# Roots of a group norm passed on through DRAM rows, for three of four groups

## Chip, cores and metric

One core of a Trainium2 chip runs the kernel. The metric is the device time of one execution in microseconds (us); lower is better.

## What is computed

Two layers (DEPTH = 2) of a hybrid decoder on 256 tokens of width 1024, in float32. Each layer normalises the stream, multiplies it by one wide input matrix, runs three token mixers in parallel (a Mamba-2 scan, sliding-window attention, forgetting attention), projects each to width 1024, merges them with sigmoid gates, multiplies by an output matrix and adds the result to the stream. The change sits at the end of the Mamba-2 mixer: its 1024 output channels, already multiplied by SiLU(z), are normalised in four groups of 256 channels, for each token by itself.

```python
SEQ = 256
SSM_GROUPS = 4

def grouped_rms_norm(y, w, groups):
    b, s, d = y.shape
    yf = y.astype(jnp.float32).reshape(b, s, groups, d // groups)
    yf = yf * lax.rsqrt(jnp.mean(yf * yf, axis=-1, keepdims=True) + NORM_EPS)
    return (yf.reshape(b, s, d) * w.astype(jnp.float32)).astype(y.dtype)
...
    y = y + d_skip.reshape(SSM_GROUPS, SSM_HEADS_PER_GROUP)[:, :, None] * xh
    y = y.reshape(b, s, SSM_INNER) * jax.nn.silu(z)
    return grouped_rms_norm(y, norm_w, SSM_GROUPS)
...
        branch = jnp.einsum('bsiw,iwd->bsid', ys, w_proj[layer])
```

## The kernel before

**Weights.** All of a layer's matrix products are made from a high and a low half of each operand, both in a rounded float32 format: three products, high by high, low by high, high by low. SP's queue brings weights in pieces of 128 partitions by 1024 values (`load_to`, L341). ScalarE rounds a piece into its high half and VectorE subtracts that to get the low half (`split`, L264 and L265); in the profile these are `hi<-raw` and `lo<-raw,hi`. Six buffers hold high halves and six low ones; a split waits until TensorE has released a buffer.

**Order of the work.** TensorE's order is written out by hand: a list of operations (`ops`), each a column block of a weight matrix, and between them small tasks written as generators. A task ends each stage with `yield D`, which says how long after the present moment its next stage may be issued, by a count of TensorE's time that the kernel keeps for itself (`clock`); `pump` issues the ripe stages, and `drain` issues all that is left of a task before an operation that needs it. Apart from the first operations, only TensorE's order is held to the program: the order on VectorE, ScalarE and GpSimd is chosen by the framework's scheduler when the program is built.

**The group norm.** The Mamba-2 output lies channel by channel in eight blocks of 128 channels (`y.xs`, block 0 to 7; block u holds channels on the partitions and 256 tokens along a row). Group g is blocks 2g and 2g + 1. For each block, `u_z` (L776 on) makes the gate z with 24 products, 256 wide, and multiplies it in: ScalarE's tanh (L782), VectorE's two products (L789, L790), ScalarE's square (L792); for every second block VectorE adds the two squares (L795) and launches `group_norm`.

`group_norm` sums the squares over channels with two products against two columns of ones (L803), which puts token on the partitions: 128 partitions, two values (one for each half of the tokens), each twice. GpSimd takes a power of -1/2 (L808), and VectorE refines the root (L810, L811, L813; tile `rs`). The root is now needed along the row of every partition. ScalarE multiplies the identity matrix by it (L816, two diagonals), and `D_GN2` later TensorE multiplies 128 x 128 ones by those diagonals (L820, tile `mx<-L,ones`), so that each partition holds all 256 roots in PSUM. VectorE multiplies both blocks by it and by the weight (L823), and `split` makes the high and low half (`y.yh`, `y.yl`).

**What comes next.** After block 7 TensorE makes the branch's gate, in two halves of 128 tokens (t = 0 and 1, 24 products each, 512 wide). VectorE adds a bias to each (L890), ScalarE takes a tanh (L891). Then comes the projection of the branch (`u_proj2`): both token halves, with the channel blocks 0 to 3 first and 4 to 7 after; for each block three products, high by high, low by high, high by low. Groups 0 and 1 are drained before its first product (`drain(3)`), groups 2 and 3 before its second half (`drain(4)`). `split_late` prepares the third branch's halves in four steps on ScalarE and VectorE (`L` of 512 values).

## Time and profile before

| | us |
|---|---|
| median of three runs | 848.38 |
| the three runs | 847.70, 848.38, 850.29 |
| span of the profiled execution | 846.0 |
| TensorE busy | 833.7 (99%) |
| VectorE busy | 642.3 (76%) |
| ScalarE busy | 511.6 (60%) |
| mean granted TensorE clock | 0.996 |

The span runs from the first to the last instruction of one profiled execution; the page gives no other time for that execution, and the timed runs are others. PE is TensorE's matmuls, PEld its weight loads, DVE VectorE, ACT ScalarE, POOL GpSimd and SP the engine that issues the weights' transfers; a `q` behind an engine's name marks its instruction queue, where transfers are issued. A row of the groups shows line, engine, operation, out<-in, shape and count, then the busy time in us and the mean ns of one, then idle time ahead of it. A row of the timeline begins with start and length in us and ends, in brackets, with the idle time ahead of it and what ended it. A row on transfers ends with the KB of each and the median us from issue to landing. Layer 0's group norm lies between 303 and 336 us of the span, layer 1's between 716 and 750.

### The profile page before, as it was taken

How to read it: one execution, taken by the hardware profiler on the slowest of the kernel's cores; microseconds unless marked ns; L12 is line 12 of the kernel's file. 1: busy time of each engine (PE TensorE's matmuls, PEld its weight loads, DVE VectorE, ACT ScalarE, POOL GpSimd, SP SyncE). 2: the span in 40 equal slices, each digit the busy share in tenths (PEclk: the TensorE clock that was granted, in tenths of full speed). 3: DMA queues.
4: the chain of work that ended last, by engine and by line, in shares of the span. 5: the costliest groups of instructions: out<-in, count | busy, mean ns of one | idle time of the engine just before them, and what ended most of it. 6: DMA issues, size and time to landing. Idle time of an engine off the chain costs nothing.

```text
span 846.0 us, 15985 instructions
## 1 busy us (share of the span) xinstructions
PE 833.7 (99%) x5964; PEld 763.4 (90%) x5964; DVE 642.3 (76%) x1403; ACT 511.6 (60%) x1004; POOL 105.7 (12%) x134
## 2 busy tenths in 40 slices
PE   8999999999999999999999999999999999999996
PEld 7989898998999998888989998899899999988896
DVE  5777997998776669656788879879968567785665
ACT  6466777665666667435555667776557667654442
POOL 6410100000140010210014001000003110121000
PEclk9999999999999999999999999999999999999999
DMA  9576565666465545748676465465755654576632
GB/s 303 160 226 197 180 199 163 197 212 184 143 188 177 181 145 189 230 147 292 206 237 218 144 204 157 145 200 182 239 172 176 174 175 152 161 236 211 212 100 76
DMA packets 126638, 158.43 MB, mean 187 GB/s; under 512 B 12784, under 2 KB 88224, under 8 KB 126560
## 3 DMA queue, kind: packets, MB, share of 16 engines
q1 hardware_dynamic: 109456, 140.79, 52.5%
q10 hardware_dynamic: 17056, 16.49, 6.3%
q8 instruction: 47, 0.77, 0.4%
q14 instruction: 31, 0.25, 0.1%
q0 software_dynamic: 48, 0.13, 0.0%
HBM read 155.22 MB, written 2.16 MB: 186 GB/s over the span
## 4 chain that ended last, share of the span: by engine, by line
PE 95%; DMA 3%; DVE 1%; ACT 0%; POOL 0%; issue 0%; SPq 0%; POOLq 0%; DVEq 0%
PE mm L96 82%; PE mx L96 9%; PE mx L100 4%; DMA raw<-in_w_in_dram 3%; DVE lo L265 0%; POOL lo L1154 0%; ACT hi L1153 0%; DVE L L470 0%; ACT L L1013 0%; DVE L L265 0%; ACT L L264 0%; POOLq L1218 0%; ACT L L215 0%; DVE L L996 0%; DVE L L1001 0%
## 5 line engine op out<-in xcount | busy, mean ns | idle before, releaser
L265 DVE TENSOR_TENSOR lo<-raw,hi 128x1024 fp32r<-128x1024 f32 x252 | 308.3, 1235 | 93.8 <-ACT hi L264 84.6
L96 PE MATMUL mm<-hi,L 128*128 128x512 f32 (+1 forms) x1344 | 373.9, 364 | 2.0 <-ACT hi L1153 1.5
L264 ACT ACTIVATE hi<-raw 128x1024 fp32r<-128x1024 f32 x252 | 263.4, 1056 | 93.5 <-PE mm L96 75.5
L96 PE MATMUL mm<-L,hi 128*128 128x256 f32 x1792 | 317.7, 278 | 0.7 <-DVE L L473 0.7
L96 PEld LDWEIGHTS mm<-L,hi 128*128 128x128 f32 x1792 | 277.7, 192 | 7.6 <-issue 3.3
L96 PEld LDWEIGHTS mm<-hi,L 128*128 128x128 f32 x1344 | 241.5, 190 | 32.5 <-issue 2.7
L96 PE MATMUL mm<-L,lo 128*128 128x256 f32 x896 | 246.4, 275 | 0.0
L96 PE MATMUL mm<-lo,L 128*128 128x512 f32 (+1 forms) x672 | 241.4, 361 | 0.6 <-POOL lo L1154 0.6
L96 PEld LDWEIGHTS mm<-L,lo 128*128 128x128 f32 x896 | 171.9, 192 | 0.2
L96 PEld LDWEIGHTS mm<-lo,L 128*128 128x128 f32 x672 | 127.3, 190 | 15.4 <-POOL lo L1154 0.8
L867 POOL TENSOR_SCALAR_AFFINE_SELECT bias<-bias 128x128 f32<-128x128 f32 x64 | 35.9, 597 | 407.5 <-DVE L L736 268.6
L561 ACT ACTIVATE pp<-pp,nm 128x128 f32<-128x128 f32 (+1 forms) x128 | 56.5, 443 | 13.5 <-DVE nm L555 13.5
L698 DVE SCALAR_TENSOR_TENSOR L<-L,vec,L 128x255 f32<-128x255 f32 (+2 forms) x96 | 46.3, 482 | 4.7 <-ACT L L695 3.4
L96 PE MATMUL mx<-L,L 128*64 128x128 f32 (+1 forms) x384 | 34.4, 314 | 0.0
L891 ACT ACTIVATE L<-L 128x512 f32<-128x512 f32 x24 | 15.1, 631 | 29.9 <-DVE L L890 29.7
L573 DVE TENSOR_SCALAR pp<-pp,rsum 128x128 f32<-128x128 f32 (+1 forms) x128 | 32.2, 316 | 0.5
L701 ACT ACTIVATE L<-L 128x256 f32<-128x256 f32 x32 | 13.3, 417 | 31.5 <-DVE L L698 25.9
L96 PEld LDWEIGHTS mx<-L,L 128*64 128x64 f32 x384 | 23.0, 136 | 9.4 <-ACT pp L561 1.3
L782 ACT ACTIVATE L<-mm 128x256 f32<-128x256 f32 x48 | 18.1, 378 | 20.8 <-PE mm L96 20.8
L590 ACT ACTIVATE L<-mx 128x512 f32<-128x512 f32 x48 | 27.0, 597 | 2.7 <-PE mx L100 2.5
L100 PE MATMUL mx<-ident,pp 128*128 128x128 f32 x192 | 26.3, 273 | 0.0
L555 DVE CUSTOM_DVE_ANT_0 pp<-mx,wmask,nsink 128x128 f32<-128x128 f32 x64 | 23.4, 412 | 1.5 <-PE mx L96 1.5
(173 smaller groups left out, 717.5 us busy)
## 6 DMA issues: line engine op xcount, KB each, us to landing
raw<-in_w_in_dram SPq DMA_DIRECT2D x200, 512.0 KB, 4.5
raw<-in_w_proj_dram SPq DMA_DIRECT2D x48, 512.0 KB, 5.5
raw<-in_w_out_dram SPq DMA_DIRECT2D x16, 512.0 KB, 4.6
L<-cumd ACTq DMA_DIRECT2D x8, 512.0 KB, 5.0
bias<-cumd ACTq DMA_DIRECT2D x16, 256.0 KB, 4.0
L<-in_gate_bias_dram ACTq DMA_DIRECT2D x12, 256.0 KB, 3.9
L<-in_x_dram SPq DMA_DIRECT2D x2, 512.0 KB, 4.9
nwb<-in_norm_w_dram SPq DMA_DIRECT2D x1, 512.0 KB, 5.3
```

What stands on the lines that cost most here:

```text
L96: nc.tensor.matmul(o, a, b, **kw)
L100: nc.tensor.transpose(o, a, i)
L264: keep(act)(hi, src, AF.Copy)
L265: keep(tt)(lo, src, hi.bitcast(F32), op=ALU.subtract)
L555: nc.vector.tensor_tensor_reduce(out=pp[:, i, sl], in0=score(p, i, b), in1=biases(p, i, b), scale=-0.125, scalar=1.0e30 if ns is None else ...
L561: act(pp[:, i, sl], pp[:, i, sl], AF.Exp, scale=-1.0, bias=nm[:, e:e + 1], accum_out=sums[:, e:e + 1])
L573: ts(pp[:, i, sl], pp[:, i, sl], rs[:, 2 * i + b:2 * i + b + 1], 0.5, op0=ALU.mult, op1=ALU.mult)
L590: act(pT, pt, AF.Copy)
L698: stt(a[:, s:S], x_[:, 0:S - s], y.vec[:, 16 * j + u:16 * j + u + 1], a[:, s:S], op0=ALU.mult, op1=ALU.add)
L782: act(halves(th), p, AF.Tanh, scale=0.5)
L867: nc.gpsimd.affine_select(out=bias[:, i, dst], in_=bias[:, i, src], compare_op=ALU.is_ge, fill=NEG, base=0, pattern=[[-1, P]], channel_mul ...
L891: act(g, g, AF.Tanh, scale=0.5)
```

## The change

Groups 0, 1 and 2 (`ROWS`) no longer make the diagonals and the products with ones. The root's two columns (one value of each pair) are written to a DRAM row of 2 x 128 values, and this row is read back onto all 128 partitions, in an SBUF tile of the kind that held the diagonals. Both transfers are issued from ScalarE's queue. Three delays take the place of `D_GN2`: `D_GNW` ahead of the write, `D_GNR` ahead of the read, `D_GNS` ahead of the product that uses it. Group 3 stays as it was.

```diff
+D_GNW, D_GNR, D_GNS, ROWS = 4.5, 3.5, 5.0, (0, 1, 2)
...
         stt(r[:, 0:4], a[:, 0:4], -3.0, r0[:, 0:4], op0=ALU.add, op1=ALU.mult)
-        rb = T("L1", [P, S])
-        for t in range(2):
-            act(rb[:, t * P:(t + 1) * P], ident, AF.Copy, scale=r[:, 2 * t:2 * t + 1])
-        yield D_GN2
-        p = pmx()
-        for t in range(2):
-            mm(p[:, t * P:(t + 1) * P], ones, rb[:, t * P:(t + 1) * P], start=True, stop=True)
+        if g in ROWS:
+            row = dr.tile([2, P], F32, name=f"gn{y.l}_{g}", tag=f"gn{y.l}_{g}")
+            rc = r[:, 0:4].rearrange("p (t two) -> p t two", t=2)[:, :, 0]
+            yield D_GNW
+            with nc.allow_non_contiguous_dma(reason="one column of roots"):
+                nc.scalar.dma_start(row.rearrange("t p -> p t"), rc)
+            yield D_GNR
+            rb = T("L1", [P, S])
+            nc.scalar.dma_start(rb, row.rearrange("t p -> (t p)").partition_broadcast(P))
+            yield D_GNS
+            scale = rb
+        else:
+            rb = T("L1", [P, S])
+            for t in range(2):
+                act(rb[:, t * P:(t + 1) * P], ident, AF.Copy, scale=r[:, 2 * t:2 * t + 1])
+            yield D_GN2
+            p = pmx()
+            for t in range(2):
+                mm(p[:, t * P:(t + 1) * P], ones, rb[:, t * P:(t + 1) * P], start=True, stop=True)
+            scale = p[:, 0:S]
         for u in (2 * g, 2 * g + 1):
             n = T("L1", [P, S])
-            stt(n, y.xs[:, u, :], y.vec[:, 80 + u:81 + u], p[:, 0:S], op0=ALU.mult, op1=ALU.mult)
+            stt(n, y.xs[:, u, :], y.vec[:, 80 + u:81 + u], scale, op0=ALU.mult, op1=ALU.mult)
             split(y.yh[0][:, :, u, :], y.yl[0][:, :, u, :], halves(n))
```

Line numbers of the changed kernel are one higher up to the root (L264 becomes L265), and 14 higher behind the norm (L823 becomes L837, L890 becomes L904); the write is L820, the read L823. On TensorE three rows a layer are gone (groups 0, 1 and 2), and nothing else moves. On SP and GpSimd nothing moves. On VectorE and ScalarE the scheduler chose another order around the norm, the same one in both layers.

First place: VectorE, layer 0, between the two weight pieces that are split behind block 6. `L_368` is `y.xs`; L790 (L791 after) is the product that multiplies the gate into block 6 or 7, `lo` a weight's low half, L795 (L796) the sum of the squares of blocks 6 and 7. Before:

```order
L789 TENSOR_SCALAR L_816_4244<-L_815_4242,mm_4217 128x256
L810 TENSOR_TENSOR sm_4267<-sm_4265,sm_4263 128x4
L790 TENSOR_TENSOR L_368_1837<-L_368_1837,L_816_4244 128x256
...
L789 TENSOR_SCALAR L_835_4314<-L_834_4312,mm_4275 128x256
L790 TENSOR_TENSOR L_368_1837<-L_368_1837,L_835_4314 128x256
L265 TENSOR_TENSOR lo_4407<-raw_4079,hi_4406 128x1024
L795 TENSOR_TENSOR L_817_4247<-L_817_4247,L_836_4317 128x256
```

After:

```order
L811 TENSOR_TENSOR sm_4253<-sm_4251,sm_4249 128x4
L812 TENSOR_TENSOR sm_4253<-sm_4253,sm_4251 128x4
L790 TENSOR_SCALAR L_814_4240<-L_813_4238,mm_4213 128x256
L814 TENSOR_SCALAR rs_4256<-sm_4253,sm_4251 128x4
L791 TENSOR_TENSOR L_368_1837<-L_368_1837,L_814_4240 128x256
L266 TENSOR_TENSOR lo_4363<-raw_4061,hi_4362 128x1024
L790 TENSOR_SCALAR L_829_4298<-L_828_4296,mm_4259 128x256
L266 TENSOR_TENSOR lo_4375<-raw_4079,hi_4374 128x1024
L791 TENSOR_TENSOR L_368_1837<-L_368_1837,L_829_4298 128x256
L796 TENSOR_TENSOR L_815_4243<-L_815_4243,L_830_4301 128x256
```

Group 2's root products (L811, L812) moved ahead of block 6's gating, and the second weight's low half moved ahead of block 7's product.

Second place: VectorE, layer 0, the norm's product of groups 0 and 1 (L823, after L837) and their low halves (`L_752`), beside the low halves of the weights that follow. Before, group 0 and group 1:

```order
L823 TENSOR_SCALAR L_819_4252<-L_368_1837,vec_658,mx_4249 128x256
L823 TENSOR_SCALAR L_820_4256<-L_368_1837,vec_658,mx_4249 128x256
L813 TENSOR_SCALAR rs_4270<-sm_4267,sm_4265 128x4
L265 TENSOR_TENSOR lo_4395<-raw_4061,hi_4394 128x1024
L265 TENSOR_TENSOR L_752_3939<-L_819_4252,L_751_3938 128x2x128
L265 TENSOR_TENSOR L_752_3939<-L_820_4256,L_751_3938 128x2x128
...
L823 TENSOR_SCALAR L_838_4323<-L_368_1837,vec_658,mx_4320 128x256
L823 TENSOR_SCALAR L_839_4327<-L_368_1837,vec_658,mx_4320 128x256
L265 TENSOR_TENSOR L_752_3939<-L_838_4323,L_751_3938 128x2x128
L265 TENSOR_TENSOR L_752_3939<-L_839_4327,L_751_3938 128x2x128
L890 TENSOR_TENSOR L_842_4358<-mm_4333,L_840_4331 128x512
```

After:

```order
L266 TENSOR_TENSOR lo_4397<-raw_4162,hi_4396 128x1024
L837 TENSOR_SCALAR L_850_4382<-L_368_1837,vec_658,L_833_4320 128x256
L837 TENSOR_SCALAR L_851_4386<-L_368_1837,vec_658,L_833_4320 128x256
L837 TENSOR_SCALAR L_859_4417<-L_368_1837,vec_658,L_835_4338 128x256
L266 TENSOR_TENSOR lo_4409<-raw_4180,hi_4408 128x1024
L266 TENSOR_TENSOR L_752_3939<-L_850_4382,L_751_3938 128x2x128
L266 TENSOR_TENSOR L_752_3939<-L_851_4386,L_751_3938 128x2x128
L904 TENSOR_TENSOR L_858_4414<-mm_4355,L_831_4305 128x512
L266 TENSOR_TENSOR L_752_3939<-L_859_4417,L_751_3938 128x2x128
L837 TENSOR_SCALAR L_860_4421<-L_368_1837,vec_658,L_835_4338 128x256
L266 TENSOR_TENSOR lo_4465<-raw_4276,hi_4464 128x1024
L266 TENSOR_TENSOR L_752_3939<-L_860_4421,L_751_3938 128x2x128
```

Both groups moved from ahead of the gate's first sum (L890, after L904) to behind the next weights' low halves; blocks 0 and 1 stand behind `lo_4409`, block 3 behind the gate's second sum and `lo_4465`. Behind these rows come `lo_4477`, the products of group 3, block 4's product, group 3's low halves, `lo_4501` and only then block 4's low half.

Third place: ScalarE, layer 0, from block 6's tanh on. L816 are the diagonals, L792 (L793) the squares. Before:

```order
L782 ACTIVATE L_815_4242<-mm_4217 128x256
L792 ACTIVATE L_817_4247<-L_368_1837 128x256
L264 ACTIVATE hi_4394<-raw_4061 128x1024
L264 ACTIVATE L_751_3938<-L_819_4252 128x2x128
L264 ACTIVATE L_751_3938<-L_820_4256 128x2x128
L816 ACTIVATE L_826_4272<-ident_71,rs_4270 128x128 x2
L782 ACTIVATE L_834_4312<-mm_4275 128x256
L264 ACTIVATE hi_4406<-raw_4079 128x1024
```

After:

```order
L783 ACTIVATE L_813_4238<-mm_4213 128x256
L820 DMA gn_2_4258<-rs_4256 128x2x1
L793 ACTIVATE L_815_4243<-L_368_1837 128x256
L265 ACTIVATE hi_4362<-raw_4061 128x1024
L783 ACTIVATE L_828_4296<-mm_4259 128x256
L265 ACTIVATE hi_4374<-raw_4079 128x1024
L793 ACTIVATE L_830_4301<-L_368_1837 128x256
L823 DMA L_833_4320<-gn_0_4101 128x256
L823 DMA L_835_4338<-gn_1_4202 128x256
L905 ACTIVATE L_834_4335<-L_834_4335 128x512
L265 ACTIVATE hi_4396<-raw_4162 128x1024
```

Group 2's write stands ahead of block 6's square, the reads of groups 0 and 1 behind block 7's square, and the rounding of their blocks has moved behind two more weight splits.

## Prediction

> **What bounds the kernel now.** I read the page first, for the span, the busy shares and the chain that ended last.
>
> ```profile
> span 846.0 us, 15985 instructions
> PE 833.7 (99%) x5964; PEld 763.4 (90%) x5964; DVE 642.3 (76%) x1403; ACT 511.6 (60%) x1004; POOL 105.7 (12%) x134
> PE 95%; DMA 3%; DVE 1%; ACT 0%; POOL 0%; issue 0%; SPq 0%; POOLq 0%; DVEq 0%
> ```
>
> TensorE is idle for 846.0 - 833.7 = 12.3 us in all, and 95% of the chain is its own work. So a matmul taken out is worth its whole length, and a wait put into TensorE's stream costs its whole length: nothing later has slack to win it back. The page gives only the span of the profiled execution; the median of the timed runs, 848.4 us, lies 2.4 us above it, and I carry this 2.4 over unchanged.
>
> Second view: the groups of TensorE's instructions, shapes kept apart, and its timeline around layer 0's group norm. Of the timeline's columns the first is the start, the second the length, both in us.
>
> ```profile
> L96 PE MATMUL mx<-L,ones 128*128 128x128 f32 x32 | 4.9, 275 | 0.0
> ...
> 314.25 0.61 PE L96 MATMUL mx<-L,ones 128*128 128x128 f32 x4
> 314.70 0.51 PE L96 MATMUL mx<-ones,L 128*128 128x2 f32 x4
> ...
> 317.83 0.61 PE L96 MATMUL mx<-L,ones 128*128 128x128 f32 x4
> 318.19 0.68 PE L96 MATMUL mm<-hi,L 128*128 128x512 f32 x2
> ...
> 323.46 0.61 PE L96 MATMUL mx<-L,ones 128*128 128x128 f32 x4
> 323.90 0.51 PE L96 MATMUL mx<-ones,L 128*128 128x2 f32 x4
> 324.27 0.68 PE L96 MATMUL mm<-hi,L 128*128 128x512 f32 x2
> ...
> 329.53 0.59 PE L96 MATMUL mm<-hi,L 128*128 128x512 f32 x2
> 329.96 0.38 PE L96 MATMUL mm<-lo,L 128*128 128x512 f32 x1
> 330.18 0.59 PE L96 MATMUL mm<-hi,L 128*128 128x512 f32 x2
> ...
> 332.12 0.61 PE L96 MATMUL mx<-L,ones 128*128 128x128 f32 x4
> ...
> 335.16 0.59 PE L96 MATMUL mm<-hi,L 128*128 128x512 f32 x2
> ```
>
> There are 32 records for 16 products (two records each), two products a group, eight groups in two layers. The first three rows of four records are groups 0, 1 and 2, the row at 332.12 is group 3, which stays. The row at 329.53 is the first product of the branch's projection, 335.16 the start of its second half; three 512-wide products take 0.65 us (329.53 to 330.18), so 0.216 each.
>
> **What is removed.** From the start of each product row to the row behind it: 0.45 (314.25 to 314.70), 0.36 (317.83 to 318.19), 0.44 (323.46 to 323.90). That is **1.25 us a layer, 2.5 us in all**, 0.30% of the time; 24 of 32 records of 4.9 us would be 3.7, but records overlap, so the starts count. The other order of TensorE's work does not change. ScalarE also loses three pairs of copies a layer (0.69 a pair); it is no bound by itself, and nothing is booked for them.
>
> **What is added, and its unknown durations.** Each of six groups gets a write of 256 separate four-byte values and a read of one 1 KB row onto 128 partitions, both on ScalarE's queue.
>
> ```profile
> L<-xres ACTq DMA_DIRECT2D x4, 128.0 KB, 4.0
> L<-xres ACTq DMA_DIRECT2D x2, 256.0 KB, 2.9
> ...
> dsk<-in_d_skip_dram ACTq DMA_DIRECT2D x4, 2.0 KB, 9.2
> cumd<-L ACTq DMA_DIRECT2D x2, 32.0 KB, 2.1
> ...
> L259 ACTq DMA_DIRECT2D dsk<-in_d_skip_dram x4: 621/646/646, 31.5 to 364.5; - x4
> ...
> L681 ACTq DMA_DIRECT2D cumd<-L x2: 324/334/344, 74.3 to 489.8; - x2
> ...
> DMA to landing us min/median/max: 2.1/4.0/5.9
> ```
>
> The write lands after between 2.1 (the row cumd, also into DRAM, long pieces) and 9.2 (dsk, 512 four-byte values, but among eleven transfers issued together). I take 5.6, halfway, since here are half as many values and alone. Issuing it holds ScalarE's sequencer 0.33 (cumd) to 0.65 (dsk); I take 0.65, the row with small pieces. The read: between 2.9 (L<-xres, 256 KB) and 5.9 (the longest of the accesses to cumd, in the last row); I take 4.0, the row of the same size. The norm's product on VectorE now reads its scale from SBUF, for 0.43 a piece (0.86 for two at 322.95 below) as before: a product of the same width from SBUF, L790, takes 0.42.
>
> Neither transfer is waited for at these values. Group 1's write, issued at 315.6, lands at 321.2, and the read behind it is reached at about 323.0: cover 1.8. Group 0's read, issued at 322.65, lands at 326.65, and VectorE reaches its product at 327.45: cover 0.8.
>
> The Trainium skill, page "DMA: Bandwidth & Descriptors", section "Specifications", asks for 512 bytes a transfer for line rate and says that smaller ones become read-modify-writes; that speaks against this write. The same page's section on the anatomy of a DMA gives about 2.0 us fixed cost, mostly the receipt of the write. The row cumd agrees with the second; by it alone the sum below stays as it is, and the first is one way into rival C.
>
> **What is moved.** This is the larger part: VectorE and ScalarE take their work in another order around the norm, and I lay the rows' durations end to end in the new order, on the clock of before. Their rows, in start and length:
>
> ```profile
> 315.58 1.01 POOL L808 TENSOR_TENSOR sm<-sm,mhalf 128x4 f32<-128x4 f32 x1 [2.63 <-DVE sm L805]
> ...
> 316.45 0.42 DVE L789 SCALAR_TENSOR_TENSOR L<-L,mm 128x256 f32<-128x256 f32 x1 [1.02 <-ACT L L782]
> ...
> 316.91 0.42 DVE L790 TENSOR_TENSOR L<-L,L 128x256 f32<-128x256 f32 x1
> ...
> 321.14 0.42 DVE L790 TENSOR_TENSOR L<-L,L 128x256 f32<-128x256 f32 x1
> 321.48 1.22 DVE L265 TENSOR_TENSOR lo<-raw,hi 128x1024 fp32r<-128x1024 f32 x1
> 322.62 0.42 DVE L795 TENSOR_TENSOR L<-L,L 128x256 f32<-128x256 f32 x1
> 322.95 0.86 DVE L823 SCALAR_TENSOR_TENSOR L<-L,vec,mx 128x256 f32<-128x256 f32 x2
> ...
> 317.42 0.42 ACT L792 ACTIVATE L<-L 128x256 f32<-128x256 f32 x1 [1.00 <-DVE sm L811]
> 317.79 1.06 ACT L264 ACTIVATE hi<-raw 128x1024 fp32r<-128x1024 f32 x1
> ...
> 321.68 0.41 ACT L792 ACTIVATE L<-L 128x256 f32<-128x256 f32 x1
> ...
> 325.39 0.63 ACT L891 ACTIVATE L<-L 128x512 f32<-128x512 f32 x1 [1.12 <-DVE L L890]
> ...
> 326.23 1.04 ACT L264 ACTIVATE hi<-raw 128x1024 fp32r<-128x1024 f32 x1
> ```
>
> *Wait 1, before group 3's sums.* Group 2's root products now stand ahead of block 6's gating product and wait for GpSimd until 316.6 (315.58 + 1.01); the gating product starts at 317.0 instead of 316.45. ScalarE then issues group 2's write (root at 317.5, 0.65 us) ahead of block 6's square, which moves from 317.42 to 318.15, and the weight split behind it from 317.79 to 318.5. On VectorE a low half of 1.14 us (start to start, 321.48 to 322.62) now stands ahead of block 7's product: 322.2 instead of 321.14. Its square runs at 322.65 instead of 321.68, and the sum of squares, done at 323.04 before, at 323.5. TensorE wanted it at 323.90 and now wants it 1.25 earlier, at 322.65: **0.9 us**. TensorE is then 0.35 ahead of before.
>
> *Wait 2, block 0's low half, the second product of the projection.* The projection starts at 329.53 - 0.35 = 329.2. Group 0 had its product at 317.32 before; now it stands behind the gate's weight splits: ScalarE's first split there at 325.2, its low half 326.3 to 327.45, three norm products to 328.65, another low half to 329.8, then block 0's low half, done at 330.2. TensorE wants it at 329.4: **0.8 us**.
>
> *Wait 3, block 3.* VectorE goes on without a gap: block 1 to 330.5, the gate's sum (0.6) to 331.1, block 2 to 331.4, block 3's norm product to 331.85, a weight's low half to 333.0, block 3's low half to 333.4. ScalarE rounds block 3 by 332.3. TensorE, 0.8 late, wants the rounded block at 331.9 (329.2 + 0.8 + 9 x 0.216) and one product later the low half: 0.4 + 0.85 = **1.25 us**.
>
> *Wait 4, block 4.* The second half starts at 335.16 - 0.35 + 0.8 + 1.25 = 336.85. Group 2 comes last of all, behind group 3 and a further weight split on each engine: ScalarE rounds block 4 by 337.05, VectorE does that weight's low half from 336.8 and block 4's by 338.4. TensorE wants them at 336.85 and, with the first 0.2 waited, 337.3: 0.2 + 1.1 = **1.3 us**.
>
> Together 4.25 us a layer. In layer 1 the same rows stand in the same new order, so 8.5 us. SP's and GpSimd's orders don't change. The sum: 846.0 - 2.5 + 8.5 = 852.0 us of span, and 848.4 + 6.0 = **854.4 us**, slower by 0.7%. With the write's issue at 0.33 the first wait loses about 0.3 a layer and all four some 0.45: 853.5.
>
> **Rivals.**
>
> *A, faster: the cover holds.* If VectorE and ScalarE run ahead of where I put them, by 0.9 us at the first wait, 0.8 at the second and 1.3 at the last, TensorE never waits, and only the 2.5 us are left: 845.9 us. For it: ScalarE sits idle for 1.0 and 1.1 us in the rows above, and the old order had every block ready in time. Against it: from 326.3 to 333.4 VectorE's new order has no gap to run ahead from.
>
> *B, about the same: part of the cover holds.* If one or two of the four waits fall away, since later waits partly repeat earlier ones, 0.9 to 2.5 us a layer stay, against 1.25 gained: 847.7 to 850.9 us. For it: each wait is some tenths beside instructions of 1.2 us. Against it: three of the four come from one instruction that plainly stands ahead, a 1.14 us low half.
>
> *C, slower still: the round trip is the wait.* A read of 5.9 puts the product 1.1 us behind VectorE's reaching it, all of which reaches TensorE: 2.2 in two layers, 856.6. A write that lands after 9.2 holds ScalarE at group 1's read from 323.0 to 324.8; its tanh and its split of the gate come 0.6 us later and the projection with them, 1.2 in two layers, 855.6. With both, group 1's read lands at 330.7 instead of the 328.25 at which VectorE wants it: 2.45 a layer, 859.3. It decides from a write over 7.4 us, or a read over 4.8. For it: the row dsk. Against it: cumd's 2.1, and that dsk waited among eleven. By the page's rule on small transfers the write would go this way.
>
> That the change does not do what it says is excluded: the three product rows a layer are gone from TensorE's order.
>
> **How the numbers follow.** Forecast (three or four of the waits, 852 to 856.5): 0.57. C (over 856.5): 0.19. B: 0.17. A: 0.07. What a measurement of this kernel can tell from no change is about 0.3%, 845.8 to 850.9 us. A lies on its edge and gives faster 0.04, the rest of it and most of B give same 0.16, and slower is 0.80. The range runs from B's upper part, 849.5, to C with both ends, 859.5; A, B's lower part and what lies over it make about 2 in 10.
>
> **What would show it.** Records of mx<-L,ones fall from 32 to 8. TensorE's idle time grows from 12.3 to about 21 us, in four places a layer: before group 3's sums, released by the sum of squares on VectorE, and before the projection's products of blocks 0, 3 and 4, released by VectorE's low halves L266. The writes land within 7 us and the reads within 4.8. If TensorE waits for a DMA, or VectorE's norm products L837 do, C was right. If no idle time stands in the projection, A was. I would be wrong at the root if the engines' new order let the weight splits run earlier than their buffers' release at 325.2 allows here.

## The result and the profile after

The changed kernel takes 871.48 us (median of 4 runs, 869.35 to 872.86), the kernel before beside it 848.04 (4 runs): a ratio of 1.0271 (1.025 to 1.0292). It is slower by 23.4 us, where 6.0 were forecast. The profiled execution's span grew from 846.0 to 870.0.

The page of the changed kernel, top lines and the chain of waits; the last two rows are its new transfers in the table of DMA issues (the last number of each is the median time from issue to landing), and the two rows behind them give least, median and longest time of the writes (first) and of the reads:

```profile
span 870.0 us, 15927 instructions
PE 839.0 (96%) x5940; PEld 763.4 (88%) x5940; DVE 643.2 (74%) x1403; ACT 508.8 (58%) x992; POOL 103.6 (12%) x134
PEclk9999999999999997999999999999999999989999
PE 43%; DVE 2%; DMA 2%; ACT 0%; issue 0%; POOL 0%; POOLq 0%; ACTq 0%; SPq 0%
L<-gn ACTq DMA_DIRECT2D x6, 128.0 KB, 6.7
gn<-rs ACTq DMA_DIRECT2D x6, 1.0 KB, 10.5
DMA to landing us min/median/max: 9.3/10.5/12.1
DMA to landing us min/median/max: 5.6/6.7/11.8
```

Three things stand there. TensorE has 24 records fewer and yet 5.3 us more busy time (839.0 against 833.7), and the row of its clock has a 7 and an 8 where it had nines throughout: some of its work ran at a lower clock. Its idle time grew from 12.3 to 870.0 - 839.0 = 31.0. And the writes land after 10.5 us, not 5.6, the reads after 6.7, not 4.0.

Where TensorE waits around the norm: its timeline in layer 0 and behind it layer 1, only rows with idle time ahead of them (the bracket: how long, and who ended it).

```profile
321.86 0.61 PE L97 MATMUL mx<-ones,L 128*128 128x2 f32 x4 [0.32 <-DVE L L796]
333.57 0.80 PE L97 MATMUL mm<-hi,L 128*128 128x512 f32 x1 [5.82 <-ACT L L265]
335.38 0.79 PE L97 MATMUL mm<-hi,L 128*128 128x512 f32 x1 [1.01 <-DVE L L266]
345.26 0.48 PE L97 MATMUL mm<-hi,L 128*128 128x512 f32 x1 [0.81 <-DVE L L266]
...
760.80 0.80 PE L97 MATMUL mm<-hi,L 128*128 128x512 f32 x1 [6.08 <-ACT L L265]
762.61 0.80 PE L97 MATMUL mm<-hi,L 128*128 128x512 f32 x1 [1.02 <-DVE L L266]
772.30 0.48 PE L97 MATMUL mm<-hi,L 128*128 128x512 f32 x1 [0.81 <-DVE L L266]
```

The wait of 5.82 us stands before the projection's first product, where the forecast had none. Follow it back: ScalarE's rounding of block 0, then VectorE's norm product L837, then a transfer. First ScalarE's timeline (ACTq rows are transfers that it issues), then VectorE's:

```profile
306.86 0.37 ACTq L820 DMA_DIRECT2D gn<-rs  x1
314.03 0.37 ACTq L820 DMA_DIRECT2D gn<-rs  x1
316.05 0.37 ACTq L820 DMA_DIRECT2D gn<-rs  x1
...
321.01 5.94 ACTq L823 DMA_DIRECT2D L<-gn  x2
326.99 0.63 ACT L905 ACTIVATE L<-L 128x512 f32<-128x512 f32 x1 [5.65 <-DMA gn<-rs]
...
333.10 1.21 ACT L265 ACTIVATE L<-L 128x256 fp32r<-128x256 f32 x3 [3.00 <-DVE L L837]
```

```profile
328.60 1.22 DVE L266 TENSOR_TENSOR lo<-raw,hi 128x1024 fp32r<-128x1024 f32 x1 [4.19 <-ACT hi L265]
332.58 1.27 DVE L837 SCALAR_TENSOR_TENSOR L<-L,vec,L 128x256 f32<-128x256 f32 x3 [2.76 <-DMA L<-gn]
```

Two delays show. At the read of group 1 (second in the row at 321.01) ScalarE waits for group 1's write, issued at 314.03, until 326.6, and the gate's tanh and a weight split, which come behind it in ScalarE's rows, start 5.65 us late. And VectorE's product waits until 332.58 for group 0's row, whose read was issued at 321.01. The read ends last: VectorE still waits 2.76 us for it after the hold of ScalarE and the split behind it are over (3.6 us in layer 1). That is the forecast's rival C by its own sign (L837 waits for a DMA), at a price that it did not have.

The third view is the stretches of 4 us around the writes. The columns of interest are the last three: clock, busy share of the DMA engines, GB/s. First the kernel before, then the changed one:

```profile
310.00:314.00 4.00, 4.00 (x39) 3.53 (x40) 3.03 (x7) 2.08 (x5) 1.19 (x1) 1.00 0.52 163
```

```profile
310.00:314.00 4.00, 4.00 (x39) 3.83 (x36) 3.08 (x10) 0.77 (x2) 1.19 (x1) 1.00 0.87 19
```

In the changed kernel the DMA engines are 87% busy and move only 19 GB/s. The weights pay for it: of SP's loads issued from 309 to 321 us the landing took 3.4 in the kernel before and 10.2 to 13.5 in the changed one.

```profile
DMA to landing us min/median/max: 3.4/3.4/3.4
```

```profile
DMA to landing us min/median/max: 10.2/10.5/13.5
```

The packets in the trace agree. A weight packet of 2 KB takes 84 ns as a rule. In the two microseconds that begin at 310 us, behind the first write's 256 pieces, the longest one on SP's queue took 7.6 us; from 304 us up to then, none took more than 1.2. The pieces themselves are recorded at 9 ns each.

Where the 24.0 us of span come from, place by place: the same product of TensorE in the two traces, start in the changed kernel minus start before (in brackets the two starts). The last column is the same for the kernel e1_row below.

| TensorE's product | change | e1_row |
|---|---|---|
| ahead of the norm of layer 0 | -1.20 | -0.85 |
| behind group 1's removed row (318.19, 316.19) | -2.01 | -1.35 |
| projection, first (329.53, 333.57) | +4.04 | -1.69 |
| second (329.75, 335.38) | +5.64 | -0.41 |
| second half, first (335.16, 343.97) | +8.81 | +1.12 |
| second half, second (335.37, 345.26) | +9.89 | +2.20 |
| behind the change of layers (387.91, 400.27) | +12.36 | +2.51 |
| layer 1, ahead of the projection (731.59, 743.17) | +11.58 | +2.88 |
| first (742.93, 760.80) | +17.87 | +2.55 |
| second (743.14, 762.61) | +19.47 | +3.84 |
| second half, second (748.77, 772.30) | +23.54 | +6.44 |

So two thirds of the loss, 6.05 + 1.60 and 6.29 + 1.60, fall at the projection's start in the two layers. From there to the second half some 3 us a layer are lost, most of it at half clock: by the trace's clock records TensorE was granted 0.5 for 10.2 us from 331.1 and for 10.2 us from 757.8. Then 1.1 a layer at the second half (1.3 forecast), and 2.5 at the change of layers, which no step of the forecast had.

### The profile page after: what moved, and what is told of

Its sections match the earlier page's. It is cut to its first block, busy times and chain, and to the rows that moved or that the text cites. A ratio compares the mean times of both kernels' runs of the same rounds, so it can differ in the third digit from the quotient of the medians.

```text
span 870.0 us, 15927 instructions
## 1 busy us (share of the span) xinstructions
PE 839.0 (96%) x5940; PEld 763.4 (88%) x5940; DVE 643.2 (74%) x1403; ACT 508.8 (58%) x992; POOL 103.6 (12%) x134
## 5 line engine op out<-in xcount | busy, mean ns | idle before, releaser
L97 PE MATMUL mm<-hi,L 128*128 128x512 f32 (+1 forms) x1344 | 378.7, 367 | 17.5 <-ACT L L265 12.2
L266 DVE TENSOR_TENSOR lo<-raw,hi 128x1024 fp32r<-128x1024 f32 x252 | 309.0, 1236 | 106.2 <-ACT hi L265 97.3
L265 ACT ACTIVATE hi<-raw 128x1024 fp32r<-128x1024 f32 x252 | 263.5, 1055 | 97.4 <-PE mm L97 73.4
L101 PE MATMUL mx<-ident,L 128*128 128x128 f32 x152 | 22.6, 275 | 2.5 <-DVE L L954 2.3
```

The source lines that it names most:

```text
L97: nc.tensor.matmul(o, a, b, **kw)
L101: nc.tensor.transpose(o, a, i)
L265: keep(act)(hi, src, AF.Copy)
L266: keep(tt)(lo, src, hi.bitcast(F32), op=ALU.subtract)
```

## The experiments

Each ratio is to the kernel before on the same chip (its medians there ran from 847.74 to 848.69). At first three theories stood against each other: S, it is the write in small pieces; D, it is a round trip through DRAM in any form; O, it is the order of VectorE and ScalarE alone.

### e1_row: the same round trip in long pieces

TensorE turns the roots into a row, which is written as two pieces of 512 bytes; the rest is the change.

```diff
-            with nc.allow_non_contiguous_dma(reason="one column of roots"):
-                nc.scalar.dma_start(row.rearrange("t p -> p t"), rc)
+            pr = pmx()
+            transpose(pr[0:2, 0:P], rc, ident)
+            rr = T("L1", [2, P])
+            act(rr, pr[0:2, 0:P], AF.Copy)
+            nc.scalar.dma_start(row, rr)
```

> The changed kernel with the write made long: TensorE transposes the two columns of roots to two rows of 128, ScalarE copies them to SBUF, and two pieces of 512 bytes are written in place of 256 of four bytes; the read is as in the change. Theory S: the write lands in 2 to 3 us, weight loads in 3.4 to 6 us, no halved clock, 850 to 857 us. Theory D: ScalarE still waits 3 us or more for a write, 862 or more. Theory O: 854 or a little more.

Measured: 854.78 us (853.61 to 855.1), ratio 1.0072 (1.0051 to 1.0093). The reads landed after 3.5 us, and TensorE's waits in layer 0 are the forecast's second to fourth, near the forecast's sizes when counted as delays (below) and with the forecast's releaser:

```profile
DMA to landing us min/median/max: 2.9/3.5/3.5
```

```profile
329.34 0.48 PE L97 MATMUL mm<-hi,L 128*128 128x512 f32 x1 [1.12 <-DVE L L266]
...
332.47 0.48 PE L97 MATMUL mm<-hi,L 128*128 128x512 f32 x1 [0.54 <-DVE L L266]
...
337.57 0.48 PE L97 MATMUL mm<-hi,L 128*128 128x512 f32 x1 [0.81 <-DVE L L266]
```

Of the change's 23.4 us 16.4 go with the form of the write alone (two pieces of 512 bytes instead of 256 of four); D is out. What is left, 7.0 us, is near the forecast's 6.0. ScalarE still waits 2.47 us for group 1's write here, and the scheduler's order is not the change's row for row: around blocks 6 and 7 VectorE works in the order of before.

### e3_readonly: no write, the reads kept

The reads fetch a row of the input x in place of the roots, so nothing waits for a write.

```diff
-            with nc.allow_non_contiguous_dma(reason="one column of roots"):
-                nc.scalar.dma_start(row.rearrange("t p -> p t"), rc)
...
-            nc.scalar.dma_start(rb, row.rearrange("t p -> (t p)").partition_broadcast(P))
+            nc.scalar.dma_start(rb, x2[0:1, 0:S].to_broadcast([P, S]))
```

> The changed kernel without its six writes: the reads stay, but fetch a row of the input x in place of the roots, so the norm's scale is not the reference's; nothing waits for a write. Theory S (small pieces: the write of 256 four-byte values holds the DMA engines for about 10 us, delays the weight loads behind it and stops ScalarE, which waits for it): the 18 us or so go with the writes, only the new order of VectorE and ScalarE is left, 850 to 856 us, weight loads around the norm land in 3.4 to 6 us, the clock stays at 1.0 there. Theory D (any way through DRAM is this slow at this place): reads still land after 6 us or more, 858 us or more. Theory O (the engines' new order costs as much as forecast, 4.25 us a layer): 853 to 855; if it comes to 846 to 848, the order costs nothing.

Measured: 857.09 us (856.57 to 858.83), ratio 1.0106 (1.0083 to 1.0128), at no lower clock around the norm. Its reads took 4.3 to 6.4 us and VectorE waited 0.4 us twice for them, so its wait before block 0 is larger than that of e1_row:

```profile
326.41 0.88 DVE L835 SCALAR_TENSOR_TENSOR L<-L,vec,L 128x256 f32<-128x256 f32 x2 [0.41 <-DMA L<-in_x_dram]
327.68 0.48 DVE L835 SCALAR_TENSOR_TENSOR L<-L,vec,L 128x256 f32<-128x256 f32 x1 [0.40 <-DMA L<-in_x_dram]
```

A read over 4.8 us does reach TensorE, as rival C had it (856.6 by its reckoning). Without the write, 14 of the 23 us are gone.

### e2_unread: the write alone, read by nobody

The kernel before, with the change's write added behind the roots of groups 0 to 2 and everything else kept.

```diff
+        if g < 3:
+            row = dr.tile([2, P], F32, name=f"gn{y.l}_{g}", tag=f"gn{y.l}_{g}")
+            rc = r[:, 0:4].rearrange("p (t two) -> p t two", t=2)[:, :, 0]
+            with nc.allow_non_contiguous_dma(reason="one column of roots"):
+                nc.scalar.dma_start(row.rearrange("t p -> p t"), rc)
```

> The kernel before, with the write of groups 0 to 2 added and read by nobody; the products with ones stay. Theory S: writes land after 9 to 12 us, weight loads issued within the same 10 us land after 8 to 13 us instead of 3.4 to 4.1, and as the high halves must wait for them the time rises to 850 to 862. Theory D and theory O: nobody waits for the write, so 848 to 851 (the scheduler's order differs a little here too).

Measured: 850.72 us (849.42 to 854.52), ratio 1.0036 (1.0019 to 1.0053). The writes landed after 10.6 to 13.5 us here too. Where nobody waits for them they cost some 3 us by the medians. The profiled execution is the longest of the ten (854.52 us); in it TensorE waits 1.0 and 0.7 us at group 3's sums (for L795) and 3.0 at the change of layers. So the writes alone are a small part of the loss; most of it comes from waiting for them.

### e9_order: the order alone, no transfers

The change without its six writes and six reads; the norm products of groups 0 to 2 read a block of x as their scale.

```diff
-            with nc.allow_non_contiguous_dma(reason="one column of roots"):
-                nc.scalar.dma_start(row.rearrange("t p -> p t"), rc)
             yield D_GNR
-            rb = T("L1", [P, S])
-            nc.scalar.dma_start(rb, row.rearrange("t p -> (t p)").partition_broadcast(P))
             yield D_GNS
-            scale = rb
+            scale = y.xs[:, 2 * g, :]
```

> The changed kernel without any of its transfers: the six writes and six reads are left out, and the norm's products of groups 0 to 2 take their scale from a block of x that lies in SBUF (so those three groups are not normalised). What is left is the removal of the ones products and the order in which VectorE and ScalarE now take their work. If the order alone gives what the kernel with 512-byte pieces lost (lag of 6.55 us at its end), it comes to 852 to 855 us, with TensorE's four or fewer waits released by L266 and none of a clock below 1 at the norm. If it is the round trip through DRAM in any form that costs, whatever the size of the pieces, this kernel is at 845 to 848, since it saves the products and waits for nothing.

Measured: 855.73 us (854.4 to 856.45), ratio 1.0088 (1.0069 to 1.0108). The waits of TensorE in layer 0, summed by releaser (total, times, longest):

```profile
PE mm L97 <- DVE L L266: 1.6, 2, 0.8
PE mm L97 <- ACT L L265: 0.8, 1, 0.8
PE mx L97 <- DVE L L796: 0.2, 1, 0.2
```

A kernel that saves the products and waits for no transfer at all loses 7.5 us: this part of the loss is the order. The scheduler's order is not the change's row for row here (two norm products stand further ahead), so the single waits differ from those of e1_row. Part of the 7.5 is a stretch of 3.4 us at half clock in layer 0, behind the two waits of 0.8.

### e11_noprod: the products left out, nothing put in their place

```diff
-        p = pmx()
-        for t in range(2):
-            mm(p[:, t * P:(t + 1) * P], ones, rb[:, t * P:(t + 1) * P], start=True, stop=True)
+        if g < 3:
+            scale = rb
+        else:
+            p = pmx()
+            for t in range(2):
+                mm(p[:, t * P:(t + 1) * P], ones, rb[:, t * P:(t + 1) * P], start=True, stop=True)
+            scale = p[:, 0:S]
```

> The kernel before without the products of ones for groups 0 to 2, and with nothing in their place: ScalarE still makes the diagonals, and VectorE's norm products read the diagonal from SBUF as their scale (so those groups are not normalised). No transfer is added. It asks what the removal alone is worth. If a product taken from TensorE is worth its length and nothing else, it is 2.5 us faster than before, 845 to 846.5 us. If removing it lets the scheduler put the norm's products and a weight's low half on VectorE in another order here too, so that TensorE waits for a low half ahead of or in the projection, the gain is given back: 847 to 850 us, with idle time of 1 to 2 us a layer released by L266.

Measured: 850.66 us (849.28 to 852.98), ratio 1.0037 (1.0024 to 1.005). Taking 2.5 us of work off the engine that is 99% busy makes the kernel 2 us slower. One wait is the order's: TensorE's sums of group 3 now wait 1.1 us for L795. The other stands at the change of layers, where TensorE's transposes wait for VectorE's L944:

```profile
389.00 0.66 PE L100 MATMUL mx<-ident,L 128*128 128x128 f32 x4 [2.55 <-DVE L L944]
```

The expectation had not named that place. It is the same instruction behind which the change lost 2.5 us and e2_unread 3.0.

### e13_noprod_dskrow and e12_dskrow: small pieces at the change of layers

Ahead of that place ScalarE's queue loads layer 1's constants, with d_skip in single four-byte values. Both kernels read it as one row of 64 bytes a partition, out of which GpSimd copies the values; e13 is e11_noprod with this edit, e12 the kernel before with it.

```diff
-        for half in range(2):
-            src = d_skip[l:l + 1, :].rearrange("o (j two) -> two o j", two=2)[half]
-            pdma(y.dsk[64 * half:64 * half + 64, :], src.to_broadcast([64, NK]))
+        dk = T("dk", [P, 2 * NK], bufs=2)
+        pdma(dk, d_skip[l:l + 1, :].to_broadcast([P, 2 * NK]))
+        for half in range(2):
+            pin(nc.gpsimd.tensor_copy)(y.dsk[64 * half:64 * half + 64, :],
+                dk[64 * half:64 * half + 64, :].rearrange("p (j two) -> p j two", two=2)[:, :, half])
```

> The kernel without the products of groups 0 to 2 and without transfers (850.66 us), with one thing altered: in the constants of a layer, d_skip is read as one row of 64 bytes for each partition in place of 512 single four-byte values, and two small copies on GpSimd pick its halves. The order of all other work is the same. Question: the 2.5 us that TensorE waits at the change of layers (its transposes, for L944), seen in five of the variants with 0.4 to 3.0 us. If it comes from small pieces, which hold up the weights that are issued behind them, the wait goes and the time falls by about 2.5 us to 847 to 849 us, weights behind the constants land after 3 to 5 us instead of 10 to 12. If it comes from the order of the work, both stay: 850 to 852.

> The kernel before with the same edit of d_skip alone. If small pieces hold up weights wherever they stand, the weights issued behind the constants (363 to 376 us) land after 3 to 5 us instead of 9.8 to 12.2. TensorE did not wait there in the kernel before, so the time is at most a little shorter: 846 to 848.5 us.

Measured: e13 847.97 us (847.27 to 850.97), ratio 1.0001 (0.9989 to 1.0013), 2.7 less than e11_noprod, and the wait for L944 is gone. e12 847.84 (847.53 to 849.16), ratio 0.9988 (0.9976 to 1.0001): the same as before, within what can be told. The weights issued from 366.5 to 378 us, in the kernel before, in e11 and in e13:

```profile
DMA to landing us min/median/max: 9.8/11.7/12.2
```

```profile
DMA to landing us min/median/max: 9.5/10.4/14.2
```

```profile
DMA to landing us min/median/max: 4.5/6.8/9.0
```

And the four microseconds from 370 us in e11, then in e13 (again clock, DMA share, GB/s at the end of the row): nothing is moved at all in the first, 290 GB/s in the second.

```profile
370.00:374.00 4.00, 4.00 (x20) 3.52 (x19) 4.00 (x5) 1.76 (x3) 0.00 (x0) 1.00 0.05 0
```

```profile
370.00:374.00 4.00, 4.00 (x20) 3.49 (x20) 3.94 (x4) 2.62 (x3) 0.00 (x0) 1.00 0.91 290
```

So the loss at the change of layers in e11 is small pieces again, of a load that was in the kernel before and cost nothing there: it held the weights up by 5 us or so, which just fitted. In the change and in eight of the other kernels TensorE waits at that place, for 0.3 to 3.0 us; in e1_row and e4_poolread it does not. Together with e11 this also prices the removal: without that stall it is worth nothing that can be told (1.0001, and 0.1 us from e12), since TensorE's sums of group 3 still wait, 0.8 us a layer, for VectorE. In the trace of e13 TensorE is ahead of the kernel before by 0.09 us at the start of layer 0's norm and by 0.29 after group 3's sums: of the 1.25 us saved, 1.05 are gone.

### e4_poolread: who is held while the write lands

```diff
-            nc.scalar.dma_start(rb, row.rearrange("t p -> (t p)").partition_broadcast(P))
+            nc.gpsimd.dma_start(rb, row.rearrange("t p -> (t p)").partition_broadcast(P))
```

> The changed kernel with its six reads issued on GpSimd's queue instead of ScalarE's; writes, products and sizes are the same. Two theories of the 8 us a layer that TensorE waits ahead of the projection. Hold: ScalarE, which is strictly in order, is held 5.6 us at group 1's read until group 1's write has landed, and the gate's tanh and the weight splits with it; on GpSimd's queue nobody on TensorE's path is behind it, so the projection starts some 5 us a layer earlier and the time is 858 to 863 us. Lateness: the roots' row itself comes late (write 10.5, then read 6.7 behind the next write in the same queue), VectorE's product of group 0 or 1 waits for it whoever issues the read, and the time stays at 866 to 872 us with L837 released by a DMA at about 331 us.

Measured: 870.98 us (868.21 to 873.86), ratio 1.027 (1.0238 to 1.0302): no gain, where Hold had promised some 10 us. The rows of GpSimd and VectorE say why. Group 0's read, issued at 317.69 as soon as its write had landed, took 13.3 us, and VectorE's product starts at 331.04. But the wait for group 1's write now holds GpSimd for 9.61 us, with group 3's root (L809) behind it, and VectorE waits 6.76 us for that root before it comes to the product.

```profile
317.69 0.62 POOL L823 DMA_DIRECT2D L<-gn  x1 [2.33 <-DMA gn<-rs]
327.92 0.55 POOL L823 DMA_DIRECT2D L<-gn  x1 [9.61 <-DMA gn<-rs]
328.49 1.03 POOL L809 TENSOR_TENSOR sm<-sm,mhalf 128x4 f32<-128x4 f32 x1
```

```profile
DMA to landing us min/median/max: 13.3/13.3/13.3
```

```profile
329.55 0.16 DVE L811 TENSOR_TENSOR sm<-sm,sm 128x4 f32<-128x4 f32 x1 [6.76 <-POOL sm L809]
331.04 0.88 DVE L837 SCALAR_TENSOR_TENSOR L<-L,vec,L 128x256 f32<-128x256 f32 x2 [0.93 <-DMA L<-gn]
```

In layer 0 the data is late by another 0.93 us after that; in layer 1 VectorE waits 7.85 us for the root and for no transfer. So the hold has only moved to another engine that TensorE depends on, and this run does not separate it from the lateness of the data. In the changed kernel itself the data ends last, as shown above; what the hold costs by itself stays open.

### e6_one: one group, the earliest

```diff
-D_GNW, D_GNR, D_GNS, ROWS = 4.5, 3.5, 5.0, (0, 1, 2)
+D_GNW, D_GNR, D_GNS, ROWS = 4.5, 3.5, 5.0, (0,)
```

> The change made for group 0 alone, two groups in all, which has the longest cover (written at about 307 us, wanted at about 327); groups 1 to 3 keep their products of ones. If what costs is the chain of write and read that ends after VectorE and ScalarE want it, and writes that come close together, one early group costs little: removing its products saves 0.8 us, the order of VectorE and ScalarE costs about 1.8 by an estimate from the rows' durations laid end to end, so 847 to 851 us, no wait of L837 for a DMA. If each write in small pieces costs by itself, through the other transfers that it delays, a third of the changed kernel's loss is seen: 854 to 857.

Measured: 850.09 us (849.04 to 851.05), ratio 1.0024 (1.0014 to 1.0033). The write still takes 9.0 to 10.3 us, but with no other write behind it its read lands after 4.2 (3.7 to 4.8), and VectorE does not wait for it: the first of the two expectations. It fits the reads of 11.8 and 13.3 in the change and in e4 being held by the pieces of groups 1 and 2, which are on their way at that time. Of the 1.8 us that are lost, 1.6 stand at the change of layers.

### e5_warm: TensorE kept busy through the wait

```diff
             drain(3)
+            idle = pmx()
+            for i in range(50):
+                nc.tensor.transpose(idle[:, 0:P], ident, ident)
```

> The changed kernel, with 50 products of the identity with itself (about 0.11 us each) put on TensorE ahead of the projection, where it was idle for 5.8 us a layer; their result is used by nobody and the order of the other engines is the same. If the clock halves because TensorE was idle: the stretches of 10.2 us at clock 0.5 disappear, the projection starts when it did, and 3 to 4 us a layer come back, 863 to 866 us. If the halved clock has another cause, such as the DMA traffic: it stays, 870 to 873.

Measured: 871.39 us (870.76 to 873.04), ratio 1.0277 (1.0251 to 1.0303). Inconclusive: in that run the roots came later still (TensorE's first product of the projection starts at 335.23 us, not 333.57), TensorE waited 2.00 and 1.33 us behind the 50 transposes, and the clock fell anyway, for 6.8 and 3.4 us instead of 10.2 twice.

```profile
327.61 5.62 PE L939 MATMUL mx<-ident 128*128 128x128 f32 x50
335.23 0.48 PE L97 MATMUL mm<-hi,L 128*128 128x512 f32 x1 [2.00 <-ACT L L265]
337.05 0.80 PE L97 MATMUL mm<-hi,L 128*128 128x512 f32 x1 [1.33 <-DVE L L266]
```

### e8_sizes and e10_spread: what makes the write slow

Both are the kernel before with six unread writes. In e8, 128 four-byte values side by side (groups 0 and 2) and 128 pieces of 16 bytes (group 1); in e10, 128 four-byte values each, 512 bytes apart (group 0), side by side (1) and 16 bytes apart (2).

```diff
+        if g < 3:
+            row = dr.tile([2, 2 * P], F32, name=f"gn{y.l}_{g}", tag=f"gn{y.l}_{g}")
+            with nc.allow_non_contiguous_dma(reason="one column of roots"):
+                if g == 1:
+                    nc.scalar.dma_start(row.rearrange("t (p k) -> (t p) k", k=4), r[:, 0:4])
+                else:
+                    nc.scalar.dma_start(row[0:1, 0:P].rearrange("t p -> p t"), r[:, 0:1])
```

```diff
+        if g < 3:
+            row = dr.tile([P, (P, 1, 4)[g]], F32, name=f"gn{y.l}_{g}", tag=f"gn{y.l}_{g}")
+            with nc.allow_non_contiguous_dma(reason="one column of roots"):
+                nc.scalar.dma_start(row[:, 0:1], r[:, 0:1])
```

> The kernel before, with its products, plus six writes that nobody reads: for groups 0 and 2 only 128 single four-byte values (half of the change's write), for group 1 128 pieces of 16 bytes. If the landing goes by the number of pieces, from some 2.1 us fixed (the row cumd) to 11.8 for 256 in the kernel with unread writes, all three land after 6 to 8 us, the 16-byte pieces no later than the four-byte ones. If it goes by bytes, 128 four-byte values land after 6 to 8 and the 2 KB of group 1 after 15 or more. If it is a fixed price of any write in small pieces, all land after 10 to 12. The time: 848 to 850.5 us, between the kernel before and the one with unread writes of 256 values (850.7).

> The kernel before, with its products, plus six unread writes of 128 single four-byte values each, that differ only in the distance at which the values land in DRAM: group 0's 512 bytes apart, group 1's side by side, group 2's 16 bytes apart. Before it, 128 four-byte values side by side landed after 9.1 to 9.8 us (group 0's place) and 128 pieces of 16 bytes after 5.9 (group 1's place). If it is neighbours in one short stretch of DRAM that hold each other up, group 0 lands after 3 to 6.5 us here, group 1 after 9 to 10, group 2 between. If it is the size of four bytes itself, whatever lies beside it, all three land after 9 to 10.5. If it was the place in the program (what else the queues move at that moment), group 1 lands after about 6 here too. The time: 848 to 850.5 us by all of them.

Measured: e8 850.28 us (849.61 to 851.25), ratio 1.002 (1.0007 to 1.0033); e10 850.17 (849.18 to 854.23), ratio 1.0025 (1.0009 to 1.0041). The landings: e8's 128 values side by side, e8's pieces of 16 bytes (one landing, in layer 1); then e10's group 0 in layer 0 (512 bytes apart) and group 1 in layer 1 (side by side), one landing each.

```profile
DMA to landing us min/median/max: 9.1/9.4/9.8
```

```profile
DMA to landing us min/median/max: 5.9/5.9/5.9
```

```profile
DMA to landing us min/median/max: 3.4/3.4/3.4
```

```profile
DMA to landing us min/median/max: 12.4/12.4/12.4
```

And the stretch behind group 0's write, in e8 and in e10:

```profile
310.00:314.00 4.00, 4.00 (x42) 3.61 (x39) 3.08 (x8) 2.04 (x4) 1.19 (x1) 1.00 1.00 47
```

```profile
310.00:314.00 4.00, 4.00 (x41) 3.76 (x35) 3.08 (x9) 1.32 (x2) 1.19 (x1) 1.00 0.47 131
```

The same 128 four-byte values in the same place of the program land after 3.4 us instead of 9.8 when they lie 512 bytes apart. They do not hold up the weights either: the load that SP issues at 310.6 lands after 3.6 us, where the two issued around that time in e8 took 10.0 and 11.9. All three rules that e8 was to tell apart fell: half the pieces land only about a microsecond sooner than 256 in the same place (9.8 against 10.6 in e2_unread), and 16-byte pieces, with four times the bytes, sooner than four-byte ones. Of e10's three, the distance is left: group 0 rules out the size alone, group 1 (12.4) the place. Group 2's write, 10.9 us at 16 bytes apart, came 1.8 us behind group 1's and says little by itself.

## Why the prediction was wrong

**The removal** was right in size on TensorE: it is ahead by 0.81 more after the first two removed rows (0.45 + 0.36 forecast). But "a matmul taken out is worth its whole length" did not hold: with nothing put in the products' place, and without the stall at the change of layers, the time is the same (e13: 1.0001), because TensorE meets the wait before group 3's sums.

**The waits that the order brings** were right as mechanism and near in size. In e1_row, where the transfers are fast, TensorE loses 1.28 before block 0's low half (0.8 forecast), 1.19 at block 3 (1.25) and 1.42 at the second half (1.3), released by L266 as forecast; the first wait, 0.9, came to 0.5 in the changed kernel (0.32 of it idle) and is absent from e1_row, whose VectorE takes block 6's gating product ahead of group 2's root again, and block 7's ahead of the weight's low half. Its 854.78 us stand beside the 854.4 of the forecast, which is in part luck: the missing first wait makes up for a second one that is larger by 0.5, and for the 0.4 a layer that the transposes take back from the removal.

**The step that failed** is "Neither transfer is waited for at these values", by the two landings under it. The read was taken at 4.0; group 0's, the one that TensorE's wait ends with, took 11.8 in layer 1, and in layer 0 VectorE's product started 11.6 us after its issue. Both go back to the form of the write (with long pieces, in e1_row, the reads land after 3.5). Of its landing the forecast says: "I take 5.6, halfway, since here are half as many values and alone". It measured 10.5, above the upper bound of 9.2 from the row dsk. Both reasons were wrong: half as many values take almost as long (e8), and dsk was not slow because it stood among eleven transfers. It was slow by its own pieces (as one row it lands after 4.5 in e12), and made others slow. The row for that stood in the trace of before: weights issued behind it landed after 9.8 to 12.2 us where those at the norm took 3.4. I read dsk's own landing and not that of its neighbours.

**From there the price of rival C was too low**, 859.3 with both ends. It took each transfer by itself, with a read of at most 5.9. But group 0's read is issued while the pieces of groups 1 and 2 are on their way: issued at 321.01, with its product released at 332.58. Put into the forecast's own chain, a product that starts at 332.58 gives block 0's rounding at 333.10 and TensorE at 333.57, where it was free at about 327.75: the 5.82 of the trace. Two such waits and the half clock that follows them make up most of what was missing. What share the half clock has by itself is not settled: it takes 3.1 us a layer between the projection's second product and its second half, but in that stretch e1_row, at full clock, loses 1.5 to its waits (from -0.41 to +1.12), so 1.6 a layer by comparison; e5_warm was to show it and did not.

**The change of layers**, 2.5 us, was in no term. In e11 the same wait is a stall that the kernel before avoided by little, as e13 shows; in the changed kernel it was not tried by itself.

Rival A (the cover holds) and B were far off; that the transfers are hidden failed with the landing times.

## What to carry to other kernels

Before a value is sent through DRAM, look in the trace for a transfer in pieces as small and as close together, and read not only its own landing but that of the transfers issued behind it on other queues. If a row is needed, make it long first (here a transpose on TensorE of 0.27 us) and write it in pieces of hundreds of bytes. And where a scheduler orders the other engines, work taken off the bound engine moves all of them: the removal alone can come out slower, so its gain is counted only after the new order has been laid out.

## What the hardware showed that was not expected

- Four-byte values side by side in DRAM, 128 or 256 of them, land after 9.0 to 14.3 us in all the kernels here, and in the changed kernel they hold up a 2 KB packet of SP's queue for 7.6 us. 512 bytes apart they land after 3.4 us and the longest weight packet behind them takes 1.0 us (one write, one landing). Reads in small pieces hold weights up too: behind d_skip's 1024 values out of 64 bytes nothing moved from 370 to 374 us in the kernel before, against 289 GB/s in e12; there the number of pieces and their size changed together. Why close addresses matter was not tried.
- The Trainium skill, page "DMA: Bandwidth & Descriptors", section "Specifications", asks for at least 512 bytes a transfer for line rate, with a read-modify-write below. The trace agrees that small pieces are slow (10.5 us for 1 KB in four-byte values). Size alone does not give the time here, since four-byte values at a distance took 3.4; whether a read-modify-write is behind either, no run here shows.
- A long wait of TensorE is followed by slow work. After idle stretches of 5.82 and 6.08 us the granted clock was 0.5 for 10.2 us. Cut into thirds of 3.4 us, TensorE was busy for 23%, 75% and 100% of them in layer 0 (from 331.1 us) and for 12%, 70% and 100% in layer 1 (from 757.8): the first third lies mostly in the wait, the second holds most of the 1.0 us for L266, and full clock came back behind the first third that was busy throughout.
- The Trainium skill, page "TensorE: Matmul & The Clock Gate", section "What's actually happening", has the clock halved after at least one idle window of some 3.4 us and back after at least one busy window of the same length. The changed kernel agrees with both. But the idle window need not be idle throughout: in e9_order the clock was 0.5 for 3.4 us from 333.5, behind 3.4 us in which TensorE was busy for 53% and no single wait was longer than 0.81 us. Why it fell there and not in e3_readonly, where TensorE was busy for 50% from 326.4 to 329.8 us, no run here shows.
